# One-hot columns as products of two short factors, and one block's expert values summed by TensorE on column tiles

## The chip, the cores and the metric

The kernel runs on one core of one Trainium2 chip. The metric is device microseconds of one execution: 3978.25 us, the median of three runs (3976.56 to 3999.44).

## What is computed

One layer of a streaming encoder over nine blocks of 128 tokens: eight of a prompt (0 to 7) and one of eight samples with 16 tokens each (SB, number 8). The layer is a mixer (RMS norm, one wide projection, chunk-band attention, a gated linear recurrence, two branch projections, an output projection) followed by PEER, a retrieval of experts. Only the second half of the reference matters for the change:

```python
def peer_tokens(xt, wq, keys1, keys2, expert_u, expert_v):
    q = (xt @ wq).reshape(t, PEER_HEADS, 2, HALF_KEY)
    s1 = jnp.einsum('thd,hnd->thn', q[:, :, 0], keys1)
    s2 = jnp.einsum('thd,hnd->thn', q[:, :, 1], keys2)
    v1, i1 = lax.top_k(s1, 16)
    v2, i2 = lax.top_k(s2, 16)
    ... # the 16 best sums of pairs: e_idx = i1 * 128 + i2, g = softmax of the sums
    act = jax.nn.gelu(jnp.einsum('thkd,td->thk', expert_u[e_idx], xt))
    return jnp.einsum('thk,thkd->td', g * act, expert_v[e_idx])
```

Every token picks 16 experts in each of 8 heads, so 128 of 16384 experts, each with a row of 1024 in `peer_u` and one in `peer_v`. All is in float32.

## The kernel before, in words

**Stages.** Three mixers run one after another, over the blocks (0, 1, SB), (2, 3, 4) and (5, 6, 7), some 24 to 621 us, 621 to 1285 us and 1285 to 2008 us of the span. Each has five stages: the recurrence's inputs (LRU), its branch projection `w_bl`, the attention with the q, k and v projections, then `w_ba` and `w_o`, and the PEER query projection `wq` with the scores. A projection (`proj`, L179) is 24 matmuls of 384 columns; its weights come as 512 KB, and from the second mixer on another 512 KB holds their low part. After the mixers comes a dense stage (`dense`, 2008 to 3977 us) that handles the experts of five blocks (DENSE: 1, SB, 2, 3, 4) by multiplying all 128 groups of experts.

**Two ways to do PEER.** For the dense blocks `build_g` writes a matrix of weights G[i1, i2, token] to DRAM. For a token it is the product of two one-hot matrices over its 128 picks: `ow` (i2 times the power of two of the gate) and `oh`, `ol` (i1 times high and low part of the gate's mantissa). One `part` makes eight tokens: five VectorE instructions over 128x1024 16-bit elements (L993 to L997: two compares with an iota, three multiplications), then 16 TensorE products (L1008, L1009) and two ScalarE copies (L1011). There are 16 parts a block; those of blocks 1 and SB run in mixer 1 and those of 2, 3 and 4 in mixer 2. `tables` (L876) prepares the indices of a block as rows over picks.

The other blocks (GATHER: 0, 5, 6, 7) fetch rows: `gather(b)` (L914) issues 128 indirect DMAs from GpSimd, each of which fetches for all 128 tokens the row of their j-th pick, 512 KB. In the first half VectorE forms the dot product with the token (`dot`, L937), in the second it adds value row times weight into `x2` (`add`, L958). Block 0's gather is run beside mixers 1 and 2, those of 5, 6 and 7 in the dense stage.

**What sets the order.** A planner in Python spreads work over the mixers: `beat(us)` (L269) is called after each projection and attention unit; it takes steps from `fill` (picks, tables, parts) at an even pace, and steps of block 0's gather from `flow` at FLOW steps a microsecond (0.13 to 0.3 by stage). One step of `rows` (L925) issues one gather and uses the row fetched three steps earlier. Engines run their queues in order; a scheduler that simulates the program fixes that order, and `after(eng)` (L199) keeps an instruction behind the last marked one on its engine. Block 0's rows share three buffers (g0 to g2). PSUM tiles of projections, transposes and one-hot products share four banks (tag `pp`).

Of the kernel before, what the change touches and what calls it, by code (L numbers as in the profile page):

```python
# [10 lines left out]
F32 = mybir.dt.float32  # L11
# [10 lines left out]
D = 1024  # L22
# [42 lines left out]
def r32(ap):  # L65
    return ap.bitcast(F32R)
# [3 lines left out]
def kernel(ctx, tc, a):  # L70
# [33 lines left out]
    V.memset(h_last, 0.0)  # L104
    st_conv = const.tile([128, 8, 8, 3], F32, name="st_conv")
    nc.scalar.dma_start(st_conv, a["st_conv"])
    st_lru = const.tile([128, 8, 8], F32, name="st_lru")
    nc.scalar.dma_start(st_lru, a["st_lru"])
    conv_s = const.tile([128, 8, 8, 3], F32, name="conv_s")
    rms = const.tile([128, NB], F32, name="rms")  # L110
    lru_s = const.tile([128, 8, 8], F32, name="lru_s")

# [3 lines left out]
    g_d = {b: dr_p.tile([128, 128], F32, name=f"g_d{b}") for b in GATHER}  # L116
    tab_d = {b: dr_p.tile([128, 320], F32, name=f"tab_d{b}") for b in DENSE}
    x2_d = {b: dr_p.tile([128, D], F32, name=f"x2_d{b}") for b in range(NB)}

    def rstd_of(ss, q_="", r=None):  # L120
        m = sm_p.tile([128, 1], F32, name="rs_m" + q_)
        V.tensor_scalar(m, ss, 1.0 / D, EPS, op0=ALU.mult, op1=ALU.add)
        if r is None:
            r = sm_p.tile([128, 1], F32, name="rs_r" + q_)
        S.activation(r, m, ACTF.Sqrt)
        V.reciprocal(r, r)
        q = sm_p.tile([128, 1], F32, name="rs_q" + q_)
        V.tensor_tensor(q, r, r, op=ALU.mult)
        V.tensor_tensor(q, q, m, op=ALU.mult)
        V.tensor_scalar(q, q, -0.5, 1.5, op0=ALU.mult, op1=ALU.add)  # L130
        V.tensor_tensor(r, r, q, op=ALU.mult)
        return r

    def ssq(x, junk, q_=""):
        ss = sm_p.tile([128, 1], F32, name="ss" + q_)
        S.activation(junk, x, ACTF.Square, accum_out=ss)  # L136
        return ss
# [35 lines left out]
    def mm3(out, l, r, first, last):  # L173
        (lh, ll), (rh, rl) = l, r
        T.matmul(out, r32(lh), r32(rh), start=first, stop=False)  # L175
        T.matmul(out, r32(lh), r32(rl), start=False, stop=False)  # L176
        T.matmul(out, r32(ll), r32(rh), start=False, stop=last)  # L177

    def proj(src, x, Tn):  # L179

        hi, lo = load_split(a[src[0]][src[1]], key=src)
        ps = ps_p.tile([128, Tn], F32, name="pp", tag="pp")
        for k in range(KT):
            mm3(ps, (hi[:, k, :], lo[:, k, :]), (x[:, 0, k, 0:Tn], x[:, 1, k, 0:Tn]), k == 0, k == KT - 1)
        return ps
# [9 lines left out]
    late_picks = {}  # L195
    flow = []
    marks = {}
# [5 lines left out]
    def mark(eng, ins):  # L203
        marks[eng] = ins.ins

    def tick(n=1):
# [41 lines left out]
    def mixer(mp, gi, t0, xn):  # L248
# [20 lines left out]
        def beat(us):  # L269
# [9 lines left out]
            if flow:  # L279
                due[1] += FLOW[gi][stage[0]] * us  # L280
                while due[1] >= 1.0:
                    due[1] -= 1.0
                    next(flow[0], None)

# [5 lines left out]

        ol = pair("ol")

        def lru_in(c):
# [77 lines left out]
        for c in range(0, KT, 2):  # L371
# [8 lines left out]
            for e in range(2):  # L380
                lru_scan(c + e, *sts[e])

        stage[0] = phase[1] = 1
# [367 lines left out]
    def table_parts(tab):  # L751
        h = tab.bitcast(F16)
        return h[:, 0:128], h[:, 128:256], tab[:, 128:192].bitcast(BF16), h[:, 384:512], h[:, 512:640]

    def select(b, q_=""):
# [96 lines left out]
        def weights():  # L852
# [15 lines left out]
            else:  # L868
# [3 lines left out]
                nc.sync.dma_start(g_d[b], gf)  # L872
                if b in GROUPS[0]:
                    flow.append(gather(b))

        def tables(ii, gf):  # L876
# [3 lines left out]
            for n, src in enumerate((ii[0], ii[1], gf)):  # L880
                T.transpose(pt[:, n, :], src, ident)
            tab = tk.tile([128, 320], F32, name="tab", tag="cand")
            i1, i2, pw, hi, lo = table_parts(tab)
# [23 lines left out]

    def gather_rows(table, ei, j, n):
        t = g_p.tile([128, D], F32, name="row", tag=f"g{j % n}")
        P.indirect_dma_start(out=t, out_offset=None, in_=table,  # L910
                             in_offset=bass.IndirectOffsetOnAxis(ap=ei[:, j:j + 1], axis=0))
        return t

    def gather(b):  # L914
# [44 lines left out]

        yield from rows(peer_v, add)  # L960
        tmp = g_p.tile([128, D], F32, name="yf", tag="g0")
# [7 lines left out]
    def build_g(gp, b):  # L969
# [4 lines left out]
        def part(c, tb):  # L974
            def go():
                if c == 0 and tb == 0:
                    make_tables(b)
                    st["t"] = gp["st"].tile([128, 320], F32, name="tab")
# [3 lines left out]
                i1, i2, pw, hi, lo = table_parts(st["t"])  # L982
                sg = st["s"]
                t = c * 32 + tb * OH_T

                def row(x):
                    return x[:, t:t + OH_T].rearrange("p (g t) -> p g t", t=2).unsqueeze(2).to_broadcast(
                        [128, OH_T // 2, 128, 2])
# [156 lines left out]
    for n, blocks in enumerate(GROUPS):  # L1145
        phase[0] = n
        if n:
            if not gp:
                gp["iota"] = iota = g_p.tile([128, OH_T // 2, 128, 2], F16, name="iota", tag="g5")
                P.iota(iota, pattern=[[0, OH_T // 2], [1, 128], [0, 2]], base=0, channel_multiplier=0,  # L1150
                       allow_small_or_imprecise_dtypes=True)
                gp["st"] = es_g.enter_context(tc.tile_pool(name="st", bufs=1, side="right", reuse_waits="tile"))
                gp["oh"] = es_g.enter_context(tc.tile_pool(name="oh", bufs=2, side="right", reuse_waits="tile"))
            for b in GROUPS[n - 1]:
# [8 lines left out]
        for b in SELECT[n]:  # L1163
            if b in AT_ONCE:
                fill.extend(late_picks[b])
            else:
                _, rest, heads = select(b)
                fill.extend(heads + rest)
    u0 = g_p.tile([128, KT, 128], F32, name="u0", tag="g5")
    nc.sync.dma_start(u0, a["peer_ut"][0])  # L1170
# [129 lines left out]
```

## Time and profile before

| | |
|---|---|
| median of three runs | 3978.25 us |
| the profiled execution | 3979.21 us, span 3977.3 us |
| mean granted TensorE clock | 0.967 |
| TensorE / VectorE / ScalarE / GpSimd busy | 92% / 77% / 41% / 35% |
| HBM traffic | 1066 MB read, 138 MB written |

A busy TensorE is counted to modelled ends of pipelined matmuls, so 92% is not a TensorE at its peak. The span falls into three mixers and the dense stage, and the shares differ much between them, so the stretches have to be read one by one.

### The profile page before, as it was taken

To read this page: it belongs to the slowest core of one execution; us is meant where nothing else is said; L and a number is where in the kernel's file an instruction comes from. 1 tells how busy PE (TensorE), PEld (TensorE's weight loads), DVE (VectorE), ACT (ScalarE), POOL (GpSimd) and SP (SyncE) were. 2 spreads that over 40 slices of the span, in tenths; PEclk is the share of its full clock that TensorE was granted. 3 is DMA by queue.
4 is the path that set the end of the run, shared out by engine and by line. 5 is a ranking of instruction groups with operands and counts; after the bars stand their busy time and mean duration, and the time that the engine had idled before them with its cause. 6 is when DMAs were issued, how large, how long until landed. Compare 5 with 4: busy or idle time off the path is not lost. (4 is left out here: it accounts for less than half of the span.)

```text
span 3977.3 us, 59539 instructions
## 1 busy us (share of the span) xinstructions
PE 3647.0 (92%) x21775; PEld 3264.7 (82%) x21775; DVE 3042.7 (77%) x6332; ACT 1618.2 (41%) x2699; POOL 1405.4 (35%) x1094
## 2 busy tenths in 40 slices
PE   8998899898998999888888889999999899999998
PEld 7877799876887987778888778888888888888887
DVE  8433357868675879987778888888877887877887
ACT  7554346556644845665532122222222222222222
POOL 0000000122221023222106555655664655655653
PEclk9999999999998999999999999999999999999999
DMA  7778887888899898879968888989888889888986
GB/s 260 253 243 317 296 283 271 327 308 269 316 385 331 294 346 292 292 281 360 379 203 308 306 287 296 320 314 343 311 305 293 322 313 332 311 304 305 331 311 233
DMA packets 470358, 1208.05 MB, mean 304 GB/s; under 512 B 41008, under 2 KB 199088, under 8 KB 467504
## 3 DMA queue, kind: packets, MB, share of 16 engines
q1 hardware_dynamic: 292496, 638.23, 45.2%
q0 software_dynamic: 147456, 536.94, 37.8%
q10 hardware_dynamic: 30112, 29.09, 2.1%
q8 instruction: 170, 2.79, 0.3%
q14 instruction: 124, 1.02, 0.1%
HBM read 1066.15 MB, written 137.94 MB: 303 GB/s over the span
## 5 line engine op out<-in xcount | busy, mean ns | idle before, releaser
L910 POOL DMA_INDIRECT row<-peer_u,ei x512 | 698.0, 1363 | 1260.5 <-DVE row L937 631.3
L910 POOL DMA_INDIRECT row<-peer_v,ei x512 | 683.3, 1334 | 828.7 <-DVE x L958 525.4
L958 DVE SCALAR_TENSOR_TENSOR x<-row,q,x 128x1024 f32<-128x1024 f32 x512 | 655.3, 1280 | 27.2 <-DMA row<-peer_v,ei 20.8
L175 PE MATMUL pp<-xd,hi 128*128 128x320 f32 x2048 | 639.8, 312 | 31.9 <-ACT wf L1043 26.9
L937 DVE SCALAR_TENSOR_TENSOR row<-row,xt 128x1024 f32<-128x1024 f32 x512 | 613.6, 1217 | 66.1 <-DMA row<-peer_u,ei 64.4
L176 PE MATMUL pp<-xd,hi 128*128 128x320 f32 x2048 | 637.5, 311 | 0.3 <-DVE xd L142 0.3
L177 PE MATMUL pp<-xd,lo 128*128 128x320 f32 x2048 | 636.8, 311 | 0.0
L175 PE MATMUL pp<-xn,hi 128*128 128x384 f32 x1344 | 477.4, 356 | 19.1 <-ACT st L1011 7.8
L1069 PE MATMUL S<-vh,wh 128*128 128x512 f32 x1280 | 410.0, 402 | 62.2 <-DVE acc L1077 54.0
L177 PE MATMUL pp<-xn,lo 128*128 128x384 f32 x1344 | 459.4, 343 | 2.1 <-DMA lo<-lo_w_in 2.1
L176 PE MATMUL pp<-xn,hi 128*128 128x384 f32 x1344 | 460.6, 343 | 0.1
L1069 PE MATMUL S<-vh,wl 128*128 128x512 f32 x1280 | 401.1, 402 | 27.6 <-DVE wl L142 27.6
L175 PEld LDWEIGHTS pp<-xd,hi 128*128 128x128 f32 x2048 | 389.9, 190 | 42.6 <-ACT wf L1043 30.7
L141 ACT CAST hi<-raw 128x1024 fp32r<-128x1024 f32 x223 | 233.8, 1049 | 429.0 <-PE pp L176 307.2
L1069 PE MATMUL S<-vl,wh 128*128 128x512 f32 x1280 | 404.0, 397 | 0.0
L176 PEld LDWEIGHTS pp<-xd,hi 128*128 128x128 f32 x2048 | 389.8, 190 | 7.2 <-DVE xd L142 0.6
L177 PEld LDWEIGHTS pp<-xd,lo 128*128 128x128 f32 x2048 | 389.2, 190 | 1.6
L142 DVE TENSOR_TENSOR lo<-raw,hi 128x1024 fp32r<-128x1024 f32 x223 | 271.9, 1220 | 150.1 <-ACT hi L141 134.8
L141 ACT CAST wh<-wf 128x640 fp32r<-128x640 f32 x128 | 93.3, 729 | 616.8 <-DVE wf L1045 583.6
L1069 PEld LDWEIGHTS S<-vh,wh 128*128 128x128 f32 x1280 | 239.3, 193 | 112.3 <-DVE acc L1077 60.9
L163 ACT CAST hi<-raw 128x1024 fp32r<-128x1024 f32 x192 | 200.4, 1047 | 296.5 <-PE pp L176 204.3
L1069 PEld LDWEIGHTS S<-vh,wl 128*128 128x128 f32 x1280 | 246.7, 194 | 84.6 <-DVE wl L142 32.7
(296 smaller groups left out, 6821.7 us busy)
## 6 DMA issues: line engine op xcount, KB each, us to landing
raw<-w_in SPq DMA_DIRECT2D x168, 512.0 KB
raw<-peer_v SPq DMA_DIRECT2D x128, 512.0 KB
raw<-peer_ut SPq DMA_DIRECT2D x127, 512.0 KB
lo<-lo_w_in SPq DMA_DIRECT2D x112, 512.0 KB
G_d<-st SPq DMA_DIRECT2D x20, 2048.0 KB
gt<-G_d SPq DMA_DIRECT2D x32, 1280.0 KB
lo_w_in<-lo SPq DMA_DIRECT2D x56, 512.0 KB
raw<-wq SPq DMA_DIRECT2D x48, 512.0 KB
```

The lines of the kernel that those rows point to most:

```text
L141: S.copy(r32(hi), src)
L142: ins = V.tensor_tensor(r32(lo), src, hi, op=ALU.subtract)
L163: S.copy(r32(hi), raw)
L175: T.matmul(out, r32(lh), r32(rh), start=first, stop=False)
L176: T.matmul(out, r32(lh), r32(rl), start=False, stop=False)
L177: T.matmul(out, r32(ll), r32(rh), start=False, stop=last)
L910: P.indirect_dma_start(out=t, out_offset=None, in_=table, in_offset=bass.IndirectOffsetOnAxis(ap=ei[:, j:j + 1], axis=0))
L937: V.scalar_tensor_tensor(u, u, 1.0, xt, op0=ALU.mult, op1=ALU.mult, accum_out=hh[:, j:j + 1])
L958: V.scalar_tensor_tensor(x2, v, q[:, j:j + 1], x2, op0=ALU.mult, op1=ALU.add)
L1069: T.matmul(po[:, m, :], r32(l[:, c1]), r32(r[:, m * 512:m * 512 + 512]), start=(n == 0 and q == 0 and (c == 0 or not held)), stop=(n == EC ...
```

## The change

It has three parts and some housekeeping.

- **One-hot columns.** An index below 128 is split in `tables` into its high three bits (`a1`, `a2`) and low four bits (`b1`, `b2`). Once for 32 tokens, `part` compares these with short iotas of 8 and of 16 entries and multiplies the gate into the 8-entry factor. The columns of eight tokens are then one multiplication each (8 x 16 = 128): three VectorE instructions over 128x1024 instead of five, and seven smaller ones (five over 256 elements, two over 512) shared by four parts.
- **Values of block 0.** Block 0's indices are also written transposed (`turned`, `eT_d`). The second half of its gather then fetches by token: one indirect DMA brings the 128 value rows of one token, pick by pick over the partitions. Four such tokens, 32 apart, make a `quad`: a short VectorE copy puts their four weight columns into a zeroed tile `z`, eight plain float32 matmuls (four column tiles of 32, two halves of 512 columns) give the four sums in PSUM, each in its own row of 32 with zeros elsewhere, and two VectorE additions over 128x512 add them to `x2`. There are 32 quads; their rows share g0, g1, g2 and the buffer `xt` of the first half.
- **The end of block 0.** What is left in `flow` after mixer 2 is now run before the dense stage rather than after it.
- **Housekeeping.** The sample states move from a pool for the whole program into one that lives in mixer 0, and their two stores are moved there from the program's end; small tiles of the norm have two buffers instead of four; the table grows from 320 to 448 words; the iotas move from buffer g5 to a pool of their own, and g5 holds the factors.

```diff
-        yield from rows(peer_v, add)
+        def values(eT):
+            zq = sel_p.tile([128, 448], F32, name="zq")
+            z, qT = [zq[:, 160 * k:160 * k + 160] for k in range(2)], zq[:, 320:448]
...
+            qs = qT.rearrange("p (i s) -> p s i", s=32)
+            got = deque()
+
+            def quad(s):
+                zs, vs = z[s % 2], [got.popleft() for _ in range(4)]
+                with after("V"):
+                    V.tensor_copy(zs.rearrange("p (i c) -> p i c", c=32)[:, 0:4, 31], qs[:, s, :])
+                for m in range(2):
+                    c1 = slice(512 * m, 512 * m + 512)
+                    po = ps_p.tile([128, 512], F32, name="po", tag="pp")
+                    with after("T"):
+                        for i in range(4):
+                            z0 = 31 + 32 * i - s
+                            T.matmul(po[32 * i:32 * i + 32, :], zs[:, z0:z0 + 32], vs[i][:, c1], start=True, stop=True,
+                                     tile_position=(0, 32 * i))
+                    with after("V"):
+                        V.tensor_tensor(x2[:, c1], x2[:, c1], po, op=ALU.add)
+
+            for s in range(32 + 1):
+                if s:
+                    quad(s - 1)
+                for i in range(4 if s < 32 else 0):
+                    t = res_p.tile([128, D], F32, name="row", tag="xt") if i == 3 else None
+                    with after("P"):
+                        got.append(gather_rows(peer_v, eT, 32 * i + s, n, f"g{i}", t))
+                    if i % 2:
+                        yield
+                yield
+                yield
...
-                V.tensor_tensor(ow, gp["iota"], row(i2), op=ALU.is_equal)
-                V.tensor_tensor(ow, ow, row(pw), op=ALU.mult)
-                V.tensor_tensor(oh, gp["iota"], row(i1), op=ALU.is_equal)
-                V.tensor_tensor(ol, oh, row(lo), op=ALU.mult)
-                V.tensor_tensor(oh, oh, row(hi), op=ALU.mult)
+                product(ow, fw, g2)
+                product(oh, fh, g1)
+                product(ol, fl, g1)
...
+                def product(o, f, g):
+                    gs, full = slice(tb * OH_T // 2, (tb + 1) * OH_T // 2), [128, OH_T // 2, 8, 16, 2]
+                    V.tensor_tensor(o.rearrange("p g (a b) t -> p g a b t", b=16),
+                                    f[:, gs].unsqueeze(3).to_broadcast(full), g[:, gs].unsqueeze(2).to_broadcast(full),
+                                    op=ALU.mult)
...
+                    for n, pairs in ((8, ((fl, a1), (fw, a2))), (16, ((g1, b1), (g2, b2)))):
+                        for o, x in pairs:
+                            V.tensor_tensor(o, gp["iota", n].unsqueeze(1).to_broadcast([128, 16, n, 2]), row(x, n),
+                                            op=ALU.is_equal)
+                    V.tensor_tensor(fw, fw, row(pw, 8), op=ALU.mult)
+                    V.tensor_tensor(fh, fl, row(hi, 8), op=ALU.mult)
+                    V.tensor_tensor(fl, fl, row(lo, 8), op=ALU.mult)
...
-            S.copy(i1, pt[:, 0, :])
-            S.copy(i2, pt[:, 1, :])
+            for n, (xa, xb) in enumerate(((a1, b1), (a2, b2))):
+                u = tk.tile([128, 128], U32, name="u", tag=("ra", "m3")[n])
+                v = tk.tile([128, 128], U32, name="v", tag="pf")
+                V.tensor_copy(u, pt[:, n, :])
+                V.tensor_scalar(v, u, 15, None, op0=ALU.bitwise_and)
+                V.tensor_copy(xb, v)
+                V.tensor_scalar(u, u, 0x70, None, op0=ALU.bitwise_and)
+                V.tensor_copy(xa, u)
...
+    while flow:
+        drip()
...
-        for _ in flow[0] if b in GROUPS[0] else gather(b):
+        for _ in () if b in GROUPS[0] else gather(b):
             pass
...
-    nc.sync.dma_start(a["conv_s"], conv_s)
-    nc.sync.dma_start(a["lru_s"], lru_s)
```

## Rows read from the trace of the kernel before

**Rows 1.** The page: busy time of the engines, and VectorE in 40 slices.

```profile
PE 3647.0 (92%) x21775; PEld 3264.7 (82%) x21775; DVE 3042.7 (77%) x6332; ACT 1618.2 (41%) x2699; POOL 1405.4 (35%) x1094
DVE  8433357868675879987778888888877887877887
```

**Rows 2.** Busy time by stage: mixer 0's `w_o`, mixer 1's attention, mixer 2, dense.

```profile
core 0: us, PE busy (x) PEld busy (x) DVE busy (x) ACT busy (x) POOL busy (x), PEclk, DMA share, GB/s
494.00:527.00 33.00, 33.00 (x192) 33.00 (x191) 18.72 (x25) 12.49 (x16) 0.00 (x0) 1.00 0.77 274
786.00:1077.00 291.00, 269.49 (x1720) 217.07 (x1719) 215.75 (x561) 178.60 (x355) 75.46 (x70) 0.96 0.86 301
...
1378.00:1451.00 73.00, 62.43 (x320) 58.76 (x319) 51.65 (x179) 28.67 (x42) 14.30 (x13) 0.93 0.96 349
1451.00:1799.50 348.50, 311.71 (x2090) 252.50 (x2089) 308.99 (x797) 214.07 (x411) 92.85 (x83) 0.95 0.85 294
1799.50:1848.00 48.50, 42.91 (x302) 40.90 (x302) 35.35 (x56) 20.84 (x28) 11.86 (x8) 0.93 0.97 368
1848.00:1890.00 42.00, 39.26 (x280) 37.12 (x278) 35.34 (x53) 23.84 (x28) 10.49 (x9) 1.00 0.94 354
1890.00:2008.00 118.00, 102.69 (x720) 97.02 (x719) 78.46 (x209) 61.65 (x88) 20.49 (x18) 0.97 0.97 370
2008.00:3977.00 1969.00, 1836.19 (x10007) 1655.14 (x10004) 1646.22 (x2462) 489.04 (x690) 1097.00 (x768) 0.97 0.85 302
```

**Rows 3.** VectorE's groups in mixer 2 (1285 to 2008 us).

```profile
L958 DVE SCALAR_TENSOR_TENSOR x<-row,q,x 128x1024 f32<-128x1024 f32 x125 | 158.9, 1271 | 11.3 <-DMA row<-peer_v,ei 11.2
...
L432 DVE TENSOR_TENSOR S<-S,bias 128x256 f32<-128x256 f32 x48 | 20.7, 432 | 1.4
```

**Rows 4.** Waits in mixer 2's attention: us in total, times, longest.

```profile
POOL row L910 <- DVE x L958: 120.1, 40, 8.8
ACT hi L163 <- PE pp L176: 52.6, 21, 4.5
...
ACT p L437 <- DVE mx L434: 22.0, 18, 3.5
...
ACT p L443 <- DVE sum L439: 17.2, 13, 2.8
PEld S L524 <- ACT p L437: 15.9, 14, 3.4
...
DVE x L958 <- DMA row<-peer_v,ei: 5.7, 4, 2.9
```

**Rows 5.** VectorE's groups in mixer 2's attention (1451 to 1799.5 us).

```profile
L958 DVE SCALAR_TENSOR_TENSOR x<-row,q,x 128x1024 f32<-128x1024 f32 x83 | 105.2, 1268 | 5.8 <-DMA row<-peer_v,ei 5.7
...
L993 DVE TENSOR_TENSOR ow<-iota,tab 128x1024 bf16<-128x1024 f16 x27 | 18.4, 680 | 0.0
...
L848 DVE TENSOR_TENSOR oh<-oh 128x512 bf16<-128x512 bf16 x8 | 3.3, 414 | 0.0
...
L848 DVE TENSOR_TENSOR oh<-oh 128x256 bf16<-128x256 bf16 x8 | 2.2, 280 | 0.0
```

**Rows 6.** The additions out of PSUM in the dense stage, min/median/max ns.

```profile
L1077 DVE TENSOR_TENSOR acc<-acc,S x98: 1200/1214/1221, 2074.2 to 3967.3; 128x1024 f32<-128x1024 f32 x98
```

**Rows 7.** TensorE in order of time in mixer 0: start, duration, count.

```profile
253.44 0.34 PE L177 MATMUL pp<-xn,lo 128*128 128x384 f32 x1
253.71 0.73 PE L582 MATMUL S<-ck,qbd 128*32 128x320 f32 x4
```

**Rows 8.** The same view later: a run of column-tile matmuls of 128 columns.

```profile
274.65 0.96 PE L598 MATMUL pp<-cv,pT 128*32 128x128 f32 x26 [0.46 <-DMA cv<-cache_v]
275.35 0.28 PE L598 MATMUL pp<-vns,pT 128*32 128x128 f32 x2
```

**Rows 9.** TensorE's groups by form in mixer 0 (24 to 621 us).

```profile
L582 PE MATMUL S<-ck,qbd 128*32 128x320 f32 x128 | 19.3, 462 | 1.5 <-DMA ck<-cache_k 1.5
```

**Rows 10.** SyncE's issues in order of time: start, duration.

```profile
91.90 0.68 SPq L1186 DMA_DIRECT2D conv_s<-conv_s  x1
```

More of the change, by code (lines that the diff above doesn't have):

```diff
@@ L134, in ssq @@
     def ssq(x, junk, q_=""):
-        ss = sm_p.tile([128, 1], F32, name="ss" + q_)
+        ss = sm_p.tile([128, 1], F32, name="ss" + q_, bufs=2)
         S.activation(junk, x, ACTF.Square, accum_out=ss)
@@ L176, in mm3 @@
         T.matmul(out, r32(lh), r32(rl), start=False, stop=False)
-        T.matmul(out, r32(ll), r32(rh), start=False, stop=last)
+        return T.matmul(out, r32(ll), r32(rh), start=False, stop=last)
     def proj(src, x, Tn):
@@ L195 @@
     late_picks = {}
-    flow = []
+    flow = deque()
     marks = {}
@@ L204, in mark, with drip @@
         marks[eng] = ins.ins
+    def drip():
+        while flow:
+            try:
+                return next(flow[0])
+            except StopIteration:
+                flow.popleft()
     def tick(n=1):
@@ L291, in mixer @@
         ol = pair("ol")
+        if samp:
+            st_conv = mp["q"].tile([128, 8, 8, 3], F32, name="st_conv", bufs=1)
+            nc.scalar.dma_start(st_conv, a["st_conv"])
+            st_lru = mp["q"].tile([128, 8, 8], F32, name="st_lru", bufs=1)
+            nc.scalar.dma_start(st_lru, a["st_lru"])
+            conv_s = mp["q"].tile([128, 8, 8, 3], F32, name="conv_s", bufs=1)
+            lru_s = mp["q"].tile([128, 8, 8], F32, name="lru_s", bufs=1)
         def lru_in(c):
@@ L381, in mixer @@
                 lru_scan(c + e, *sts[e])
+        if samp:
+            nc.sync.dma_start(a["conv_s"], conv_s)
+            nc.sync.dma_start(a["lru_s"], lru_s)
         stage[0] = phase[1] = 1
@@ L873, in weights, with turned @@
                 if b in GROUPS[0]:
+                    ef = tk.tile([128, 128], F32, name="ef", tag="sh")
+                    V.scalar_tensor_tensor(ef, ii[0], 128.0, ii[1], op0=ALU.mult, op1=ALU.add)
                     flow.append(gather(b))
+                    fill.insert(min(TAB_LATE, len(fill)), lambda: turned(ef))
+        def turned(ef):
+            pt = ps_p.tile([128, 4, 128], F32, name="tr", tag="pp")
+            with after("T"):
+                T.transpose(pt[:, 0, :], ef, ident)
+            eT = tk.tile([128, 128], I32, name="eT", tag="m1")
+            V.tensor_copy(eT, pt[:, 0, :])
+            nc.sync.dma_start(eT_d[b], eT)
         def tables(ii, gf):
@@ L906, in finish, with gather_rows @@
         nc.sync.dma_start(a["y"][b], x2)
-    def gather_rows(table, ei, j, n):
-        t = g_p.tile([128, D], F32, name="row", tag=f"g{j % n}")
+    def gather_rows(table, ei, j, n, tag=None, t=None):
+        if t is None:
+            t = g_p.tile([128, D], F32, name="row", tag=tag or f"g{j % n}")
         P.indirect_dma_start(out=t, out_offset=None, in_=table,
@@ L977, in go @@
                     make_tables(b)
-                    st["t"] = gp["st"].tile([128, 320], F32, name="tab")
+                    st["t"] = gp["st"].tile([128, 448], F32, name="tab")
                     nc.sync.dma_start(st["t"], tab_d[b])
@@ L1148 @@
             if not gp:
[L1149 to L1151 removed]
                 gp["st"] = es_g.enter_context(tc.tile_pool(name="st", bufs=1, side="right", reuse_waits="tile"))
+                for k, m in ((8, 16), (16, 1)):
+                    gp["iota", k] = gp["st"].tile([128, k, 2], F16, name=f"iota{k}")
+                    P.iota(gp["iota", k], pattern=[[m, k], [0, 2]], base=0, channel_multiplier=0,
+                           allow_small_or_imprecise_dtypes=True)
                 gp["oh"] = es_g.enter_context(tc.tile_pool(name="oh", bufs=2, side="right", reuse_waits="tile"))
@@ L1168 @@
                 fill.extend(heads + rest)
+    while flow:
+        drip()
     u0 = g_p.tile([128, KT, 128], F32, name="u0", tag="g5")
```

57 lines of the change are left out of this document (37 added, 20 removed).

## The prediction

> **What bounds the kernel now.** I read the page first [rows 1]: TensorE is busy for 92% and VectorE for 77%, and the slices show VectorE rising to nines just where the mixers end. So the shares have to be taken by stage, which the view of busy time by stretch does [rows 2]. In the dense stage (1969 of 3977 us) TensorE is at 93% of the stretch; the change leaves its instructions alone, and I carry it over unchanged. What can move lies in the mixers, in mixer 2 above all. There the reader is to see three different limits. In the attention (348.5 us) VectorE is busy for 309.0 us, 89%, and TensorE for 311.7. In `w_bl`, `w_ba`, `w_o` and `wq` (281.5 us together) the DMA engines are at 0.94 to 0.97 and move 349 to 370 GB/s, with VectorE at 66 to 84%. And TensorE is never far off: 89% in the attention, 86 to 93% in the others.
>
> Is VectorE the bound of that attention? The waits [rows 4] say: in part. ScalarE waits for VectorE inside the softmax for 22.0 + 17.2 = 39 us, but for 52.6 us it waits for TensorE to be done with the last weights, and TensorE waits for the softmax's result for 15.9 us. The same stage of mixer 1 is the better witness [rows 2]: there VectorE is busy for 74%, and TensorE still stands idle for 21.5 of 291 us, 7.4%, against 36.8 of 348.5 us, 10.6%, in mixer 2. Fifteen points less VectorE go with three points less idle TensorE.
>
> **One-hot columns.** Before, a part is five VectorE instructions of 0.68 us [rows 5], 3.4 us; the other four forms have the same size and time. After, three of them stay, 2.04 us, and four parts share five instructions over 256 elements and two over 512. VectorE has 16-bit instructions of these sizes at 0.280 and 0.414 us [rows 5], so 5 x 0.28 + 2 x 0.414 = 2.23 us, 0.56 a part. A part falls from 3.4 to 2.6 us, which gives back 0.8 x 48 = 38 us of VectorE in mixer 2 and 0.8 x 32 = 26 us in mixer 1. The ten new small instructions of a table are at most 0.28 us each: 2.8 us a block, 8 in mixer 2 and 6 in mixer 1. The price of a product is bounded above by one element a cycle, which a float32 addition of 1024 elements shows, 1.21 us [rows 6]; a part would then cost 4.2 us, and the sign turns. I take 0.68, since the old multiplications read an operand with repeated pairs of two as well.
>
> **Values of block 0, VectorE.** The adds are 128 at 1.27 us [rows 3], 163 us, 125 of them in mixer 2. They become 64 additions of 512 columns out of PSUM. The rows hold 256 columns at 0.432 [rows 3] and 1024 at 1.21 us [rows 6]; a straight line between them gives 0.69 (bounds 0.43 and 1.21). With a copy of four columns at 0.15 (taken as half of the 0.28 of [rows 5], an upper end being that 0.28) a quad costs 1.53 us, 32 of them 49 us: 114 us less. In the attention alone 83 adds, 105 us, become 21 quads, 32 us. With 27 parts at 0.8 us, VectorE falls there from 309 to 309 - 73 - 22 = 214 us, 61%.
>
> **Values of block 0, TensorE.** This is what the change puts on the fuller engine. A quad is eight float32 matmuls of 512 columns, each of which runs as two records. In mixer 0 the run of column-tile matmuls of 128 columns begins 26 records between 274.65 and 275.35 us [rows 8]: 27 ns a record with four tiles at work together. Four times the columns give 108 ns, 16 records 1.72 us. Entering the small tiles costs something: the first starts 0.27 us after the last full-size matmul [rows 7], where full-size ones start every 33.0 / 192 = 0.172 us [rows 2]. With 0.1 us on either side a quad is 1.93 us and 32 are 62 us. The other end comes from the 320-column matmuls, 128 records in 19.3 us [rows 9]: 0.151 us each, 0.241 at 512 columns, 4.1 us a quad, 130 us in all. I take the lower end, because those arrive in two halves by two transfers and only two tiles run at a time, while a quad has four rows that were fetched together.
>
> One rule of the Trainium skill speaks for a dearer quad (TensorE: Matmul & The Clock Gate, "Measured speedup vs the span model"): four small tiles together were measured there at 3.07 times the speed of one, not at four. By it the 1.72 us would be 2.24 us, an estimate from that page, and 32 quads 17 us more. The page's figure is for row tiles; [rows 8] show four column tiles at the full rate, and nothing below uses the page's.
>
> Where do the quads lie? The adds of mixer 2 are 83 in the attention and, of the other 42 counted there, about 8 in `w_bl` and 34 from `w_ba` on (GpSimd runs 8, 9 and 18 there) [rows 2, 3, 5]; divided by four, some 21, 2 and 9 quads, 40, 4 and 17 us of TensorE, against 36.8, 10.6 and 23.6 us in which it stood idle [rows 2]. A quad depends on nothing that TensorE makes and nothing soon depends on it, so it can fall into such holes, but it sits in an in-order queue and needs its z copy and four rows. I take half: 31 us hidden, 31 us paid (bounds 0 and 62).
>
> **What is given back.** Attention of mixer 2: between mixer 1's idle share (3.2% of 348.5 us, 11 us) and all the idle, 37 us; I take 24, the middle. TensorE's clock there is granted at 0.95 on average [rows 2], so a tenth of the stretch ran at the lower of its two levels, which cost some 17 us; fewer holes may spare a third, 6 us. The last three stretches are held by transfers, whose bytes don't change: a quarter of 23.6 us idle, 6 us. Mixer 1 loses 20 us of VectorE at 74%; at the rate of the attention (24 us for 95) that is 5 us.
>
> **The rest.** Gathers: still 128 transfers of 512 KB. GpSimd now issues four in a row once a quad has let go of its buffers, behind nothing of its own, and the next quad is due four planner steps later, some 17 us in the attention (348.5 us for 83 adds). Before, rows three steps ahead kept VectorE waiting for only 5.7 us in the attention [rows 4], so I cost this at nothing; without that cover TensorE would stand, which is a rival below. GpSimd's 120 us of waiting for the adds goes to waiting for TensorE and holds up nothing. The end of block 0 before the dense stage: one late quad and the norm, 2 us. The moved stores cost nothing: the scheduler already issued conv_s at 91.9 us, inside mixer 0 [rows 10]. State loads and norm buffers: nothing to 3 us, ahead of the first projections' own loads.
>
> **Sum.** 3979.2 - 24 - 6 - 6 - 5 + 31 + 2 = 3971 us, against the execution that was profiled, which is 1 us above the median shown: **3970 us**. About 1% (40 us) is what a measurement here can tell from no change, so my likeliest case is no change.
>
> **The rivals.**
> - *VectorE was the bound.* A busy TensorE is counted to modelled ends, so it has more room than 10%, and the quads slip in. Then the attention gives back all 37 us and the 17 us of clock, the last stretches and mixer 1 12 us each, and a quarter of the quads is paid, 16 us: with the 2 us of the end that is -60 us, 3918 us. For it: VectorE at 89% and ScalarE's 39 us. Against it: mixer 1's idle at 74%, and the 52.6 us that ScalarE waits for TensorE.
> - *Quads hold up TensorE's queue (slower).* Each waits for a z copy traced right ahead of it, behind whatever VectorE is doing (1.27 us for one dot or add before), and with it wait all later projections. At 1.3 us a quad and nothing hidden that is 62 + 42 = 104 us against 41 given back: +65 with the end, 4043 us. It decides from (41 + 40) / 32 = 2.5 us net a quad, so from 0.6 us of waiting on top of 1.93 with nothing hidden. For it: in-order queues and late rows under DMA at 0.97. Against it: the 17 us between quads, and the scheduler that sees the copy.
> - *The products don't keep two elements a cycle.* A part costs 4.2 us, VectorE's relief in mixer 2 falls from 144 to 68 us, mixer 1 loses; giving back half, 20 us, against 33: 3991 us. Against it: the same repeated pairs at 0.68 us [rows 5]. The Trainium skill (Vector Engine (DVE) Microarchitecture Reference, "Performance modes — why throughput varies by op and dtype") tells of one element at a time where an operand repeats a single element; here pairs repeat, and the trace's own rows bear out the fast rate.
>
> **How the numbers follow.** Forecast (3945 to 3995 us) 0.60, VectorE as bound (3900 to 3938) 0.22, queue held up (4020 to 4060) 0.12, slow products (3980 to 4005) 0.06. Faster by over 1% is the second case, 0.22; slower the third, 0.12; within 1% the other two, 0.66. For eight in ten the range takes the forecast, slow products, half of the second and a little of the third: 3918 to 4014 us.
>
> **What would show it.** In the changed profile: the adds of 128x1024 gone from mixer 2, and VectorE near 60% in its attention; products at 0.68 us; records of 512 columns on 32-wide tiles that start some 0.1 us apart in fours; TensorE's waits for `zq` or a `row` under 10 us in all; `w_ba` to `wq` still at DMA 0.95 and as long as before; a dense stage of 1969 us. I am wrong if the attention of mixer 2 shrinks by more than 40 us, or if quads take over 2.5 us of TensorE.

## The result

The changed kernel takes **4042.0 us** (median of four runs, 4040.6 to 4047.0), the kernel before 3977.8 us beside it: a ratio of 1.016 [1.012, 1.019], 64 us slower. The prediction was 3970 us with a range to 4014, so it was wrong, on the slow side. The profiled execution of the changed kernel has a span of 4040.8 us, and its rows are these.

The page of the changed kernel, busy time of the engines:

```profile
PE 3728.6 (92%) x22289; PEld 3291.8 (81%) x22289; DVE 2892.9 (72%) x6334; ACT 1624.7 (40%) x2689; POOL 1361.4 (34%) x1095
```

VectorE lost 150 us of work, TensorE gained 82 us [rows 1]. Busy time by stage, mixer 2's `w_bl`, attention, `w_ba`, `w_o` and `wq`, then the dense stage:

```profile
core 0: us, PE busy (x) PEld busy (x) DVE busy (x) ACT busy (x) POOL busy (x), PEclk, DMA share, GB/s
1381.70:1469.50 87.80, 64.30 (x345) 59.33 (x344) 43.45 (x170) 28.07 (x40) 13.86 (x14) 0.84 0.81 285
1469.50:1866.70 397.20, 360.86 (x2433) 259.63 (x2431) 230.50 (x802) 218.74 (x405) 85.15 (x84) 0.95 0.74 262
1866.70:1919.00 52.30, 47.73 (x333) 42.72 (x333) 26.83 (x58) 21.32 (x28) 7.52 (x8) 0.93 0.91 338
1919.00:1963.50 44.50, 44.50 (x310) 39.16 (x308) 23.10 (x46) 21.47 (x27) 7.80 (x9) 1.00 0.95 353
1963.50:2080.00 116.50, 110.07 (x804) 97.74 (x802) 57.41 (x202) 63.84 (x93) 14.99 (x16) 0.97 0.91 348
2080.00:4040.80 1960.80, 1834.77 (x10006) 1656.27 (x10004) 1642.98 (x2458) 488.62 (x688) 1079.62 (x768) 0.97 0.86 304
```

Against [rows 2] the reader sees where the 64 us are: the attention of mixer 2 took 397.2 us instead of 348.5 (+49), `w_bl` 87.8 instead of 73.0 (+15), `w_ba` and `w_o` some 3 us more each; `wq` and the dense stage took 1.5 and 8 us less. VectorE is down to 58% of the attention, from 89%. And TensorE's idle time in that attention is 397.2 - 360.9 = 36.3 us; before, it was 36.8. All 49 us are busy TensorE. That the two idle times agree is chance: of the 36.3 us, 16.1 stand ahead of quads (the last two rows of the next view), and other waits have shrunk.

Behind the attention it is otherwise. In `w_ba`, `w_o` and `wq` the quads' matmuls keep TensorE busy for 19.2 us, yet the three together are only 5 us longer than before (213.3 for 208.5), and TensorE's idle time in them fell from 23.6 to 11.0 us.

Waits in that attention (1469.5 to 1866.7 us; total, times, longest):

```profile
POOL row L944 <- PE po L1019: 293.2, 24, 19.4
ACT hi L158 <- PE pp L171: 53.5, 27, 4.8
DVE x L1022 <- PE po L1019: 39.5, 21, 8.9
ACT pT L468 <- PE pt L467: 34.7, 20, 5.9
...
DVE oh L1090 <- PE pg L1110: 26.6, 11, 5.6
DVE S L541 <- PE S L538: 26.1, 13, 7.5
...
ACT oa L136 <- PE pp L552: 14.0, 9, 4.4
...
PE po L1019 <- issue: 9.0, 2, 7.7
...
PE po L1019 <- DVE zq L1012: 7.1, 2, 3.7
```

ScalarE and VectorE now wait for TensorE all through the stage's other work: 53.5 + 34.7 + 26.6 + 26.1 + 14.0 = 155 us in the five largest entries, the additions of the quads not among them. Before, the same five made 81 us, 52.6 of them ScalarE's wait for the last weights [rows 4]. The waits for the softmax that stood behind it [rows 4] have dropped to under 10 us each.

In `w_bl` one wait had no place in the prediction: TensorE stands 18.6 us, once, for `q`. `values` has to turn block 0's weights (`T.transpose(pt, q, ident)`, L1003) before the first quad, and `q` is the end of a chain of VectorE and ScalarE steps. The instruction sat in TensorE's queue ahead of the projection `w_bl`, which waited with it; the second line below is that projection going on. TensorE in order of time:

```profile
1420.46 0.48 PE L1003 MATMUL tr<-ident,q 128*128 128x128 f32 x1 [18.64 <-DVE q L989]
1420.59 0.67 PE L170 MATMUL pp<-xn,hi 128*128 128x384 f32 x1
```

The prices of single instructions were as predicted. VectorE's groups in the attention, with busy time, mean ns and idle time ahead:

```profile
L1022 DVE TENSOR_TENSOR x<-x,po 128x512 f32<-128x512 f32 x42 | 28.5, 683 | 39.9 <-PE po L1019 39.5 <-issue 0.2
L1090 DVE TENSOR_TENSOR ow<-fac 128x1024 bf16<-128x1024 bf16 x27 | 18.4, 684 | 0.0
...
L1080 DVE TENSOR_TENSOR fac<-iota,tab 128x512 f16<-128x512 f16 x7 | 2.9, 419 | 0.0
...
L1082 DVE TENSOR_TENSOR fac<-fac,tab 128x256 bf16<-128x256 bf16 x7 | 2.0, 285 | 0.0
```

A product takes 0.684 us, a small compare 0.28 to 0.42 us. And a quad, in TensorE's order of time:

```profile
1554.56 1.35 PE L538 MATMUL S<-kT,qT 64*128 64x320 f32 x6
1555.84 1.93 PE L1019 MATMUL po<-row,zq 128*32 128x512 f32 x16
1557.69 0.77 PE L467 MATMUL pt<-ident,p 128*128 128x128 f32 x5
```

The 16 records of this quad, which nothing disturbs, take 1.93 us, the predicted figure to the digit. Not every quad was so. All records of quads in the attention (busy time, mean ns, idle time of TensorE ahead of them):

```profile
L1019 PE MATMUL po<-row,zq 128*32 128x512 f32 x336 | 56.9, 669 | 17.9 <-issue 9.0 <-DVE zq L1012 7.1 <-ACT st L1113 1.7
```

These are 21 quads, which the working put at 40 us. All 32 take 79.9 us, 2.5 each, where it had 62. The trace places the 18 us: some 12 are in quads that were taken apart, some 6 in four that ran while a lower clock was granted (both below).

So the working priced an undisturbed quad rightly, all of them 18 us too low, and missed by 72 us. The experiments ask what the other terms did: the part of the quads that was to hide in TensorE's idle time, the waits that were costed at nothing, and the time that a freer VectorE was to give back.

### The profile page after: what moved, and what is told of

It is laid out like the page before. It is cut to its first block, busy times and chain, and to the rows that moved or that the text cites. A ratio compares the mean times of both kernels' runs of the same rounds, so it can differ in the third digit from the quotient of the medians.

```text
span 4040.8 us, 60553 instructions
## 1 busy us (share of the span) xinstructions
PE 3728.6 (92%) x22289; PEld 3291.8 (81%) x22289; DVE 2892.9 (72%) x6334; ACT 1624.7 (40%) x2689; POOL 1361.4 (34%) x1095
## 5 line engine op out<-in xcount | busy, mean ns | idle before, releaser
L944 POOL DMA_INDIRECT row<-peer_u,ei x512 | 687.7, 1343 | 1296.0 <-DVE row L971 561.3
L944 POOL DMA_INDIRECT row<-peer_v,ei x384 | 525.0, 1367 | 396.0 <-DVE x L992 280.3
L992 DVE SCALAR_TENSOR_TENSOR x<-row,q,x 128x1024 f32<-128x1024 f32 x384 | 493.6, 1285 | 10.7 <-DMA row<-peer_v,ei 4.6
```

Source lines behind the costliest of these rows:

```text
L944: P.indirect_dma_start(out=t, out_offset=None, in_=table, in_offset=bass.IndirectOffsetOnAxis(ap=ei[:, j:j + 1], axis=0))
L992: V.scalar_tensor_tensor(x2, v, q[:, j:j + 1], x2, op0=ALU.mult, op1=ALU.add)
```

## The experiments

Two theories stood at the start. **A: TensorE is the bound.** Its idle time is no room for more work, the quads are paid in full, and VectorE's relief gives little back. **B: the order is the bound.** The quads would fit, but they, their `z` copy and the turning of `q` sit badly in in-order queues. For every run the ratio is to the kernel before on the same chip; microseconds made from a ratio are the ratio times 3978.

**The two parts alone.** The changed kernel with the 128 additions of before put back, and the changed kernel with the five one-hot instructions of before put back:

```diff
e1_onehot_only
...
-        if early:
+        if False:
             eT = sel_p.tile([128, 128], I32, name="eT", tag="ei")

e2_values_only
-                product(ow, fw, g2)
-                product(oh, fh, g1)
-                product(ol, fl, g1)
+                V.tensor_tensor(ow, gp["iota"], row(i2), op=ALU.is_equal)
+                V.tensor_tensor(ow, ow, row(pw), op=ALU.mult)
...
```

> The changed kernel with block 0's values as before (128 row gathers by pick, 128 VectorE adds), so of the change only the one-hot products, the housekeeping and the earlier end of block 0 are left. Theory A (the quads are paid for in full on TensorE and bring waits of their own, the one-hot products only help): 3955 to 3972 us, attention of mixer 2 some 335 to 345 us. Theory B (the one-hot products or the new buffers cost the time): 4000 us or more.

> The changed kernel with the old one-hot columns (five instructions a part, table of 320 words, long iota in g5), so only the values of block 0 by token and TensorE are left of the change. Theory A: slower than the whole change by what the products give back, 4045 to 4065 us. Theory B: 3970 to 4000 us.

Measured: one-hot alone 3980.9 us, ratio 1.000 [0.999, 1.001]; values alone 4041.1 us, ratio 1.015 [1.013, 1.017]. The first time is in neither theory's range: the products cost nothing, but they don't help either. The second is just under A's range for the same reason. The whole loss is the values' part. The one-hot part takes 64 us from VectorE in the parts, 49 us net of the tables' new instructions (3042.7 us busy before, 2993.4 in this run), and gives nothing that can be measured; the housekeeping and the earlier end of block 0 are in the same run and show no cost. Its attention in mixer 2:

```profile
1463.50:1800.80 337.30, 310.47 (x2093) 252.05 (x2092) 293.07 (x822) 214.56 (x405) 89.04 (x83) 0.95 0.86 304
```

That stage is 11 us shorter than before in this execution, yet the span is 3979.4 us: mixer 0, which has no one-hot work, took some 10 us more (in the changed kernel, with the same housekeeping, 3 us more). So much one execution differs from another, and the ratio over all runs is what counts.

**Relief of VectorE without any quad.** The kernel before, with block 0's 128 value additions made on 320 of the 1024 columns (the rest of those sums is left out), which takes some 94 us from VectorE (0.73 us from each):

```diff
-            V.scalar_tensor_tensor(x2, v, q[:, j:j + 1], x2, op0=ALU.mult, op1=ALU.add)
+            c = 320 if early else D
+            V.scalar_tensor_tensor(x2[:, 0:c], v[:, 0:c], q[:, j:j + 1], x2[:, 0:c], op0=ALU.mult, op1=ALU.add)
```

> The kernel before, with the 128 value adds of block 0 over 320 of 1024 columns (the other 704 columns of block 0 stay without values): about 0.73 us less VectorE in each, 94 us in all, nothing added on TensorE, transfers as they were. This measures what VectorE's relief alone is worth. Theory A (VectorE is not the bound of mixer 2, as the one-hot part's 64 us for nothing suggest): 3968 to 3981 us. Rival (VectorE bounds the attention): 3920 to 3950 us.

Measured: 3964.0 us, ratio 0.996 [0.994, 0.998], 16 us faster, a little more than theory A allowed and far from the rival. Its attention, in an execution of 3954.1 us:

```profile
1449.00:1776.40 327.40, 307.00 (x2095) 247.88 (x2094) 252.55 (x797) 216.68 (x411) 85.82 (x83) 0.96 0.88 313
```

This is what less VectorE does: TensorE's idle time in the attention falls from 36.8 to 20.4 us, and that is about the whole gain, a sixth of the work taken away. VectorE was busy for 89% there and was not the bound.

**The length of the quads.** Each quad's matmuls twice (block 0's sums come out doubled), and each quad on its first 512 columns only (the second half of the sums is left out; both additions stay and add the first half's sums):

```diff
e5_double_quads
-                        for i in range(4):
+                        for r, i in [(r, i) for r in range(2) for i in range(4)]:
...
                             z0 = 31 + 32 * i - s
-                            T.matmul(po[32 * i:32 * i + 32, :], zs[:, z0:z0 + 32], vs[i][:, c1], start=True, stop=True,
+                            T.matmul(po[32 * i:32 * i + 32, :], zs[:, z0:z0 + 32], vs[i][:, c1], start=(r == 0), stop=(r == 1),

e4_half_quads
                 for m in range(2):
                     c1 = slice(512 * m, 512 * m + 512)
+                    if m == 0:
...
```

> The changed kernel with every matmul of a quad done twice into the same PSUM tile (the sums of block 0 come out doubled), VectorE, transfers and waits as they were: 512 more records, some 57 us more of TensorE. Theory A (TensorE time of quads is paid in full, no holes take it): 4092 to 4110 us. Rival (the cost of the quads is their waits for rows and z, and TensorE has holes for the matmuls): 4042 to 4065 us.

> The changed kernel with only the first half of a quad's matmuls (512 of the 1024 columns); both VectorE additions read that half's sums, so the second half of block 0's values is left out. VectorE, transfers and waits stay as they were; TensorE loses 256 records, some 28 us. Theory A (TensorE time of quads is paid): the doubling cost 38 us for 57, so 19 to 28 us less than the changed kernel, 4012 to 4024 us. Rival (a fixed price per quad, the switch to small tiles and the waits): 4030 to 4042 us.

Measured: doubled 4080.8 us, ratio 1.026 [1.023, 1.029], 39 us above the changed kernel; halved 4011.2 us, 1.009 [1.007, 1.011], 27 us (by ratios) to 31 us (by medians) below it. Doubling adds 57 us to the time of the quads' records and halving takes 25 away. The attention of the two:

```profile
1477.00:1908.30 431.30, 396.41 (x2770) 270.77 (x2768) 232.06 (x802) 218.44 (x406) 83.16 (x84) 0.95 0.70 241
...
1473.60:1845.90 372.30, 340.65 (x2265) 251.33 (x2263) 228.28 (x802) 218.57 (x405) 80.83 (x84) 0.96 0.78 277
```

Doubled (first line), the stage is 34 us longer than after with 35.6 us more of busy TensorE; halved, 25 us shorter with 20 us less (its profiled execution, 4022.7 us, was its slowest). TensorE's time is paid there in full. In the total it is not: of the doubled quads' 57 us 39 were paid, and the time lies between A's range and the rival's. The dense stage was 17 us shorter in that execution, for a reason that no run shows, and the three stretches behind the attention grew by 10 us for 15 us of added records. The halved quads came out just under A's range.

**The waits.** First the turning of `q` moved behind the first four gathers, just ahead of the first quad:

```diff
e3_turn_q_late (the transposition and its copy, moved)
             for s in range(32 + 1):
+                if s == 1:
+                    turn_q()
                 if s:
                     quad(s - 1)
```

> The changed kernel, with the transposition of the 128 weights q issued just ahead of the first quad instead of right behind the instructions that make q. In the changed kernel TensorE stood 18.6 us in front of it. Theory A (that wait is paid, since everything on TensorE stands behind it): 4022 to 4030 us, w_bl of mixer 2 back to some 73 us. Rival (w_bl is held by transfers, which go on meanwhile, so the wait is made up later): 4036 to 4044 us.

Measured: 4037.2 us, ratio 1.017 [1.013, 1.021]: 5 us by the medians, nothing by the ratios, as the rival had it. `w_bl` was 80.8 us long, 7 less, and the attention grew by 2. Then `q` turned in the first step, and the `z` copy a step of the planner ahead of its quad; and the same with the quads' matmuls free to move in TensorE's queue:

```diff
e6_z_early (turn_q as above, at s == 0, behind the gathers)
             def quad(s):
-                with after("V"):
-                    V.tensor_copy(zs.rearrange("p (i c) -> p i c", c=32)[:, 0:4, 31], qs[:, s, :])
...
                 yield
+                if s < 32:
+                    with after("V"):
+                        V.tensor_copy(z[s % 2].rearrange("p (i c) -> p i c", c=32)[:, 0:4, 31], qs[:, s, :])
                 yield

e7_quads_free (as e6, and)
-                    with after("T"):
+                    with nullcontext():
                         for i in range(4):
```

> The changed kernel with the transposition of q behind the first four gathers, and each quad's z copy issued one planner step ahead of its matmuls. Theory A: TensorE's waits in front of q (18.6 us) and of z (some 7 us) go, of which the late transposition alone gave back 5 us: 4028 to 4036 us. Rival (the waits in front of quads are for rows, not for z): as with the late transposition alone, 4036 to 4040 us.

> The kernel with early z, and the quads' matmuls no longer held behind the last marked projection, so that the scheduler may place them where its simulation sees TensorE free. Theory A (the mixer's TensorE has no holes to put them in; what looks like idle is waiting that the quads only shift): 4028 to 4040 us. Rival (the placing behind projections is what makes the quads cost): below 4015 us.

Measured: 4020.8 us, ratio 1.012 [1.009, 1.015], and 4027.3 us, 1.012 [1.009, 1.015]. What e6 takes away of the waits for `q` and `z` is worth 16 us by the ratios and 21 by the medians, more than its theory A had; TensorE still stands 9.4 us for `q` in it, and 4.0 us for rows. Where the quads stand in the queue is worth nothing more that the second run could tell; its rival, below 4015 us, did not come. The rows of e6, `w_bl` and attention:

```profile
1376.50:1459.40 82.90, 69.57 (x345) 61.12 (x345) 43.98 (x171) 28.16 (x40) 13.89 (x14) 0.90 0.88 303
1459.40:1844.00 384.60, 362.78 (x2434) 257.08 (x2432) 230.00 (x802) 217.62 (x405) 86.52 (x84) 0.96 0.78 273
```

TensorE idles 21.8 us in this attention, as in the kernel with the short additions (20.4), and is busy for 56 us more than there. That is the comparison the study turns on: with the waits ahead of quads gone but for those 4 us, the freer VectorE does shorten TensorE's idle time in the attention by 15 us, and the quads, 62.6 us of records there, fill none of what is left.

**Quads of next to no length.** As e6, with one group of four matmuls on 64 columns and one addition on 64 columns a quad (the other columns of block 0's sums are left out):

```diff
-                for m in range(2):
-                    c1 = slice(512 * m, 512 * m + 512)
-                    po = ps_p.tile([128, 512], F32, name="po", tag="pp")
+                for m in range(1):
+                    c1 = slice(0, 64)
+                    po = ps_p.tile([128, 64], F32, name="po", tag="pp")
```

> The kernel after with q turned late and the z copy one step early (as e6), and each quad cut to its first 64 of 1024 columns: four matmuls of 64 columns and one addition of 64 columns instead of eight and two of 512 (the other columns of block 0's sums are left out). Everything else of the change stays: gathers by token, four rows per step, eT, z copies, the one-hot products, the end of block 0. TensorE keeps some 0.4 us of 1.95 us a quad (estimate from the quads' records after). Theory A (quads' TensorE time paid in full, waits for q and z worth 21 us, VectorE's relief worth 16 us, nothing else in the change costs anything): e6's 4020.8 less 50 us of TensorE less a few us for the adds = 3963 to 3975 us, about e8's 3964. Rival (fetching by token in fours, the added transposition or the late end of block 0 has a cost of its own of 15 us or more): 3980 to 3995 us. Rival 2 (a quad's cost is its switch between tile sizes and its place in the queue, not its length): over 3995 us.

Measured: 3980.2 us, ratio 0.999 [0.997, 1.001]. Its attention:

```profile
1463.40:1807.70 344.30, 324.21 (x2263) 258.82 (x2261) 206.75 (x781) 217.10 (x405) 81.66 (x84) 0.95 0.82 300
```

By the ratios this is 51 us below e6 (by the medians 41): the length of the quads costs 40 to 50 us of the 64. It is also 12 us above the short additions' 0.996 (16 by the medians), at the lower edge of the rival's range. But a cut quad was not as cheap as the 0.4 us estimated: its eight records are busy for 0.63 us, 20.2 us in the run and 15.2 in this attention. The stage is 17 us longer than with the short additions, and TensorE idles as long in both (20.1 and 20.4 us). So what is left of the quads is enough for the 12 us. The run doesn't exclude that gathering by token has a part in it.

**Quads kept in one piece.** In the trace after, some quads are taken apart. TensorE in order of time:

```profile
1583.62 1.90 PE L1019 MATMUL po<-row,zq 128*32 128x512 f32 x4
1585.46 0.33 PE L467 MATMUL pt<-ident,p 128*128 128x128 f32 x1
1585.71 1.90 PE L1019 MATMUL po<-row,zq 128*32 128x512 f32 x4
...
1589.30 1.90 PE L1019 MATMUL po<-row,zq 128*32 128x512 f32 x4
1591.13 1.34 PE L538 MATMUL S<-kT,qT 64*128 64x320 f32 x4
1592.40 1.90 PE L1019 MATMUL po<-row,zq 128*32 128x512 f32 x4
```

Sixteen records that run together take 1.93 us; here each four of them take 1.90 us by themselves, one behind the other, and this one quad costs 7.6 us of TensorE. Two more shed one such piece each, two broke into six and ten records and four into halves. Two runs tried to keep the matmuls together by one uninterrupted section, of four (a half) or of eight (a quad):

```diff
e12_halves_whole (as e6, and)
-                    with after("T"):
+                    with after("T"), tc.tile_critical():
                         for i in range(4):

e13_quads_whole (as e6, with both halves in one section)
+                with after("T"), tc.tile_critical():
+                    for m in range(2):
+                        for i in range(4):
...
```

> The kernel of e6 (q turned late, z copy one step early) with the four matmuls of each half of a quad kept together in TensorE's queue (64 groups of four, nothing between). Why: in the trace after, a few quads are taken apart: at 1583.62, 1585.71, 1589.30 and 1592.40 us four matmul records each run one behind the other, 0.43 us apart, 1.85 us a piece, where a whole quad runs its 16 records four at a time in 1.9 us. In e6 TensorE's time from the record before to the record behind the quads' pieces is 106.5 us; with 64 whole halves it would be 64 x (0.26 + 0.47 + 0.52) = 80 us at most, with whole quads 68 us. Theory A (taking quads apart costs TensorE some 20 us, and TensorE's time is paid in full): 3996 to 4008 us. Rival (pieces fall into idle time or the kept-together quads wait longer for their last row, which gives it back): 4015 to 4025 us, as e6's 4021.

> As e12_halves_whole, with all eight matmuls of a quad kept together (32 groups of eight) and both additions behind them. Theory A: TensorE's time around the quads falls from e6's 106.5 to about 68 us plus waits for rows, so 3988 to 4004 us; a quad then costs the 1.93 us of the prediction, and what stays above the kernel before is the quads' 62 us less the 16 us of VectorE's relief, less what hides. Rival (the longer atomic piece waits for its last row and for two free PSUM banks at once, and TensorE stands for it): 4015 to 4040 us.

Measured: 4250.4 us, ratio 1.067 [1.064, 1.069], and 4170.6 us, 1.046 [1.043, 1.049]; both theories missed by far. The pieces are whole, but TensorE stands idle ahead of them: for 145 us in the first run and 102 us in the second, against 4 us in e6. The profile names as releasers mostly transfers that no quad reads (weights, tiles of the mixer), so what such a section waits for is not shown. Two quads of e13:

```profile
1605.45 3.64 PE L1012 MATMUL po<-row,zq 128*32 128x512 f32 x16 [5.13 <-DMA raw<-w_in]
1626.30 1.92 PE L1012 MATMUL po<-row,zq 128*32 128x512 f32 x16 [0.43 <-issue]
```

and its attention, 71 us longer than e6's, with 11 us more of busy TensorE:

```profile
1471.40:1926.90 455.50, 374.03 (x2431) 263.11 (x2429) 228.69 (x802) 217.10 (x405) 81.32 (x84) 0.88 0.66 228
```

So what taking apart costs stays unmeasured; counted from the records it is about 12 us in the changed kernel (7.6 - 1.9 for the quad shown, 1.9 for each of the two that shed a piece, 1.0 for each of the two in six and ten records, 0.2 for each in halves). What the runs do show is how dear waits ahead of a quad are: with these 102 and 145 us the times lie 150 and 230 us above e6. In the changed kernel TensorE stood 18 us ahead of quads and 18.6 us for `q`, and e6 got 16 to 21 us back; so theory B has a part, the smaller one.

No version ran faster than the kernel before without leaving work out.

## Why the prediction was wrong

**The step that failed first** is "I take half: 31 us hidden, 31 us paid". In the attention, where 21 of the 32 quads lie, next to nothing was hidden: e6's is 57 us longer than that of the short additions, for 62.6 us of quads. By its terms the forecast had this stage 10 us shorter (20 paid, 24 and 6 given back); it came out 49 us longer, 59 of the 72 us that were missed. Doubling and halving the quads moved it by +34 and -25 us for about +36 and -20 us of busy TensorE, and cutting them to 64 columns took 41 to 51 us from the total. The same term was also sized too low: the quads were to take 62 us of TensorE and took 79.9.

The argument was that a quad can fall into one of TensorE's holes, since nothing hangs on it. But with the quads and few waits the holes are 21.8 us (e6), and without any quad 20.4 (short additions). Before, they were for the most part TensorE's waits for the softmax and for ScalarE's copies of one-hot products (`st`):

```profile
PE S L524 <- ACT p L437: 12.4, 11, 3.2
PE pt L453 <- ACT st L1011: 8.0, 8, 3.3
PE pp L175 <- ACT st L1011: 6.3, 5, 4.1
```

An in-order queue meets such a wait wherever it comes, and a quad that stands ahead of other work delays that work by its length. This reading fits the runs; none of them tests it by itself. A row that pointed to it was in hand: ScalarE waited 52.6 us for TensorE [rows 4], longer than for VectorE. Behind the attention the step did better: there 19 us of quads made the stretches 5 us longer.

**The second** is the relief of VectorE, 24 + 6 + 6 + 5 = 41 us. Without any quad, 94 us less of VectorE brought 16 us; one-hot's 64 us (49 net) brought 0 ± 5. The sign that was read rightly, mixer 1's idle at 74% of VectorE, bounded the gain in the attention from below at 11 us, and the idle time fell by 15 to 16 us where nothing else waited. Taking the middle between 11 and 37, and then adding the clock and four more stretches, was too much.

**The third** is waits costed at nothing. The prediction named the queue behind a `z` copy and made a rival of it, at 1.3 us a quad. In fact TensorE waited for the copy twice, 7.1 us, and stood twice more before a quad for 9.0 us that the profile puts to no releaser; the larger wait was one the sum did not have: the turning of `q`, 18.6 us once. What e6 took away of them gave back 16 to 21 us. Every instruction of the added code that an in-order engine issues had to be listed, and this one was in the changed source though not in the shortened diff.

Put one behind the other, the runs give 25 us less given back (16 for 41), 26 to 32 us more for the quads (e6 is 57 to 63 us above the short additions, where 31 were to be paid) and 16 to 21 us of waits: 67 to 78 us, against a miss of 72. As these are differences along one chain of runs they had to add up; that is no check of its own. By stage the miss is some 59 us in the attention, 13 in `w_bl`, 2 behind the attention and 9 ahead of `w_bl`, less 10 in the dense stage, which nothing in the prediction explains.

Of the rivals, the slower one gave 4043 us, a microsecond from what was measured, and for half the right reason. "Nothing hidden" was right for the attention. Its wait of 1.3 us a quad was not (42 us against 16 to 21), and its 41 us given back were too many (16); the two errors nearly cancel. So its 4043 us is in part luck. Its turning point, 2.5 us net a quad, was nearly reached: the changed kernel's 78 us above the short additions are 2.4 us a quad, and with less given back the point itself lay lower, at (16 + 40) / 32 = 1.75 us. VectorE as the bound is refuted by the short additions, slow products by 0.684 us.

**The signs.** VectorE near 60% in the attention (58%), products at 0.68 us, and adds of 128x1024 gone: as predicted. "Records some 0.1 us apart in fours": on average yes, but four start within 0.03 us and the next four 0.43 us later. Waits for `zq` or a `row` under 10 us: 7.1 us, so this sign spoke for the forecast while the 18.6 us for `q` went unlisted. Quads over 2.5 us of TensorE were to show it wrong: they took 2.5 on average and 2.7 in the attention. `w_ba` to `wq` as long as before: within 6 us, at a DMA share of 0.91 to 0.95 instead of 0.94 to 0.97. Dense: 1961 us for 1969. The transfers were no cause: in the attention their share fell from 0.85 to 0.74, and TensorE waited 0.2 us for a row. Nor were the PSUM banks that the quads share with the projections: TensorE waited 0.5 us ahead of the attention's projections for a quad's addition.

The prediction weighed a rule of the Trainium skill (TensorE: Matmul & The Clock Gate, "Measured speedup vs the span model") by which four small row tiles together reach 3.07 times one. Here a piece that runs alone takes 1.90 us and four together 1.93 us, so these column tiles ran at 3.9 times, and leaving the rule out of the sum was right.

## What to carry to other kernels

Before moving work from one engine to another, ask of the receiving one not only how long it idles but whether anything waits for it. In this attention ScalarE and VectorE waited 81 us for TensorE in five entries while it idled 36.8, and added TensorE work was paid in full; in the stretches behind it part of it was not. A busy share of 89% on the relieved engine is no promise either; the cheap test is to shorten its work in the kernel before, here 94 us less for 16 us gained. And list every instruction that the new code puts into an in-order queue, one-time ones above all, each with what it needs and what stands behind it.

## What the runs showed of the hardware

A wait can cost TensorE twice. The quad at 1627.29 us came behind a wait of 3.38 us and took 3.62 us instead of 1.93; by stretch, an undisturbed quad, the wait, and the quad behind it:

```profile
1555.80:1557.80 2.00, 2.00 (x18) 0.53 (x18) 1.85 (x5) 0.00 (x0) 0.00 (x0) 1.00 0.74 251
1623.90:1627.20 3.30, 0.01 (x1) 0.00 (x0) 3.18 (x12) 0.98 (x2) 0.00 (x0) 1.00 0.34 134
1627.20:1631.00 3.80, 3.71 (x17) 0.79 (x18) 2.74 (x9) 0.00 (x0) 0.00 (x0) 0.55 0.02 4
```

The granted clock (the third column from the end) is at its upper level, 2.4 GHz, in the first stretch, and close to the lower level, 1.2 GHz, while the quad behind the wait runs. Three more quads of this trace were slow: behind waits of 7.68 and 3.75 us they took 4.13 and 2.71 us, and one that followed 2.4 us after a wait of 4.76 us took 3.21. One behind 1.30 us took its usual 1.92. In e13 the quad behind 5.13 us of waiting took 3.64 us likewise, and the clock of that attention averaged 0.88.

A float32 matmul of 512 columns on a 32-wide column tile is two records 0.43 us apart, and four tiles cost no more than one if they stand together in the queue (1.93 us against 1.90). Ahead of a quad of the changed kernel the first record starts 0.27 us after the last full-size one, where full-size ones start every 0.17 us, and the next full-size one starts 0.52 us after the quad's last record. The Trainium skill (TensorEngine Tiling (Array Packing), "Key Properties") says that a change of the tiling mode drains TensorE; these two gaps agree with it, about 0.1 us at either end.
